# The seam ahead of attention reordered, and both groups of scores side by side in five passes

## The chip, the cores and the metric

The kernel runs on one core of a Trainium2 chip. The metric is the device time of one execution in microseconds (us), the median of three runs. A core has these engines: PE (matrix products and transposes), ACT (ScalarE), DVE (VectorE), POOL (GpSimd) and SP (SyncE, which here issues transfers). PEld is PE's loading of weights. PE writes its results into PSUM, eight banks of 128 x 512 fp32; ACT and DVE read them there.

## The reference

It is a two-layer decoder trunk on 512 positions of width 1024 in fp32. The layer ahead is a short gated convolution with a SwiGLU feed-forward block. Then one shared pair of keys and values is projected, and the second layer is attention over a sliding window of 128 positions with sinks, followed by another SwiGLU block. Only the parts around the change:

```python
kv = rmsnorm(h, kv_norm) @ w_kv                    # 4 key heads and 4 value heads of 64
k_sh, v_sh = jnp.split(kv, 2, axis=-1)
k_sh = partial_rotary(k_sh, cos, sin)
q = partial_rotary(rmsnorm(h, b_pre_norm[j]) @ b_w_q[j], cos, sin)      # 16 heads of 64
scores = einsum('bnqhgd,bnkhd->bnhgqk', qb, kk) / sqrt(64)              # window of 128
scores = where(valid, scores, -1e30)
probs = softmax(concatenate([scores, sink]))[..., :-1]
attn = einsum('bnhgqk,bnkhd->bnqhgd', probs, vv) @ b_w_o[j]
h = h + rmsnorm(attn, b_post_norm[j])
ff = swiglu(rmsnorm(h, ffn_pre_norm[l]), ffn_w_gate_up[l], ffn_w_down[l])
h = h + rmsnorm(ff, ffn_post_norm[l])
```

## The kernel before

**Products.** Every fp32 operand is split into a high and a low part, and every product is made as three (`mm3`, L191 to L194: low with high, high with high, high with low). So a step of the contraction is a group of three matmuls. The sequence is worked on in four tiles of 128 positions (t = 0 to 3), and in two halves of 256 columns (hf) where the positions lie along the free axis. The model's width is eight chunks of 128 (f or k = 0 to 7).

**Order.** In the stages around the change all engines run exactly the order in which the code is written (`tc.manual_schedule`). Waits between engines are added by the framework from what each instruction reads and writes. Buffers of PSUM come from three pools: `ps_mm` (four banks, handed round in turn), `ps_sc` (two) and `ps_pt` (two).

**The seam.** `close` (L869) makes the down projection that ends the first feed-forward block (`ffn(0)`). While the last half of the last tile is worked on (`pmix`, four k, twelve matmuls), it does two of the four k, then the transposes of the first two tiles, then the other two k. The residual update `res` follows each tile: `res.norm(t)` (L326) makes the normalised rows `xn` on ACT; `res.turn(b, ts)` (L328) transposes on PE the chunks b and b+4 of the tiles ts into one bank (`xt`, L337), a bank for each b of 0 to 3 and each half hf; `res.split(n, f, hf)` (L340) makes the high part on ACT (`xhi`, L350) and the low part on DVE (`xlo`, L351) from that bank, for the keys and values (n = 0) and, with another gain, for the queries (n = 1). For f < 4 and n = 0 both lie in a tile named `xhl`. Chunks f and f+4 therefore are read from the same bank, `banks[f % 4, hf]`.

`last_tile` (L909) orders ACT and DVE around the last tile's update; its list `pieces` says which splits (n, f) of the first half stand at which of five places in it. The fourth place is ahead of `res.norm(3)`, the fifth behind it. Then PE projects keys (`pk`) and values (`pv`) over k = 0 to 7 for the first half, and turns the second half's tiles (2, 3) behind k=6 and k=7; those transposes go into the banks from which the first half's splits read.

**Attention.** It runs in ten passes i = 0 to 9, each through the steps of the string `ORDER`, software-pipelined: S0 and S1 are the two groups of scores of pass i (`scores(half)`, two tiles of positions each), each twelve matmuls on half of the array's rows (`psc`, L1306), M their maxima, E exponents, N normalising; T, P, L turn the probabilities of the pass before (`pt`, L1363) and split them, W weighs the values (`po`), O is the output; Q projects the queries two passes ahead (`pq`), R- rotates them (L1244 to L1248), H- splits them into `rhl` (L1253 on ACT, L1254 on POOL); K and k rotate and split the second pair of key heads (`rhi`, `rlo`; only in passes 2 and 3); Z and z multiply with the output weights (`pe`). A step name with a minus belongs to the instance started a pass earlier. Pass i starts with S0; in the profile these starts are at 548.58, 556.35, 568.60, 580.59, 592.58, 604.58, 622.01 and 634.00 for i = 0 to 7.

Of the kernel before, what the change touches and what calls it, by code (L numbers as in the profile page):

```python
# [44 lines left out]

EARLY_IN, REST_IN = 2, 0
ORDER = (
    "R- S0 T0 T1 O- Q0 M0 Q1 Z0 P0 P1 S1 T2 T3 L0 Q2 L1 G K M1 E00 E01 H- k g0 Q3 P2 P3 E10 E11 Z1 z0 W0 L2 L3 A A A N0 W1 W2 N1 W3 g1 z1"
)
STEP = {  # L50
    "S": "scores", "M": "maxima", "E": "exponents", "N": "normalise", "T": "turn", "P": "high",
    "L": "low", "W": "weigh", "O": "out", "Q": "project", "R": "rotate", "H": "split",
# [21 lines left out]
def yoco_kernel(  # L74
# [32 lines left out]
    ps_mm = ctx.enter_context(tc.tile_pool(name="ps_mm", bufs=4, space=PSUM))  # L107
# [448 lines left out]
    for l in range(2):  # L556
# [3 lines left out]
        for rd, (f0, f1) in enumerate(ROUNDS[:-1]):  # L560
            k = slice(f0 // 2, f1 // 2)
# [304 lines left out]
        if square:  # L866
            res.square(t)

    def close(ws, x, k0, res, ahead, then=None, each=2):  # L869


        n = len(x) - k0

        def part(ps, t, half, ks):
            unit(ps, t, ws[len(ws) // 2 * half :], x, ks, n, k0)

        begun = [bank("pmix", ps_mm) for _ in range(2)]
        for half in range(2):
            part(begun[half], 0, half, range(n - 1))
            for _ in range(each if half == 0 or each > 1 else 0):  # L880
                ahead.one()
        for t in range(NB):
            for half in range(2):
                if t == 0:
                    ps = begun[half]
                    part(ps, t, half, range(n - 1, n))
                else:
                    ps = bank("pmix", ps_mm)
                    if (t, half) == (NB - 1, 1):
                        part(ps, t, half, range(2))  # L890
                        for b in range(4):
                            res.turn(b, (0, 1))
                        part(ps, t, half, range(2, n))
                        for f in range(4):
                            res.split(0, f, 0)
                        res.square_mix(t, 0)
                        res.square(NB - 2)
                        res.scale(t, 0)
                    else:
                        part(ps, t, half, range(n))  # L900
                res.take(t, half, ps)
                if (t, half) != (NB - 1, 0):
                    res.square_mix(t, half)
            if t < NB - 1:
                tile_done(res, t, square=t < NB - 2)
            if t == 0 and then:
                then()
# [56 lines left out]
    def ffn(l, before, ahead, gain, gpres, following):  # L964
# [220 lines left out]
        if gpres:  # L1185
            ahead = Ahead(following)
            with tc.manual_schedule(engines=ALL):
                close(ws, acts[-1], 0, res, ahead)
            return res, ahead
        with tc.manual_schedule(engines=ALL):  # L1190
            for t in range(NB):
# [88 lines left out]
    class Heads:  # L1280
# [11 lines left out]
        def scores(self, half):  # L1292
            khi, klo = ks[self.t // 4]
            qhi, qlo = qs[self.t].hi, qs[self.t].lo
            self.pss[half] = pss = [bank("psc", ps_sc) for _ in range(2)]
            for i, cc in self.spans(half):
                n = 2 * half + i
                q = slice(n * P, (n + 1) * P)

                kk = slice(max(n - 1, 0) * P, max(n + 1, 2) * P)  # L1300
                cc = slice(i * 256, (i + 1) * 256)
                rows = [slice(e * HD, (e + 1) * HD) for e in range(2)]

                for i, (x, y) in enumerate(((qhi, klo), (qhi, khi), (qlo, khi))):
                    for e, r in enumerate(rows):
                        nc.tensor.matmul(pss[e][:, cc], x[r, q], y[r, kk], start=i == 0,  # L1306
                                         stop=i == 2)
# [118 lines left out]
    at = []  # L1426

    with tc.manual_schedule(engines=ALL):
        last_tile(res, [[(0, 4)], [(0, 5)], [], [(0, 6), (0, 7), (1, 0), (1, 1)],
                        [(1, f) for f in (4, 5, 2, 3, 6, 7)]])  # L1430
        for hf in range(2):
            c = slice(hf * 256, (hf + 1) * 256)
            for k in range(KT):
                kk = slice(k * P, (k + 1) * P)
                for ps, (whi, wlo) in zip(pk, wk):
                    mm3(ps[:, c], whi[:, kk], wlo[:, kk], xkv[k][0][:, c], xkv[k][1][:, c],
                        k == 0, k == KT - 1)
                values(2 * hf, k)
                values(2 * hf + 1, k)
                if hf == 0 and k >= 6:  # L1440
                    for b in (2 * k - 12, 2 * k - 11):
                        res.turn(b, (2, 3))
                        res.split(0, b, 1)
            if hf == 0:
                for f in range(4, KT):
                    res.split(0, f, 1)
            if hf == 0:
                ahead.one()
                for f in range(KT):
                    res.split(1, f, 1)  # L1450
                ahead.one()
                qs[0].w, qs[1].w = ahead.ready[4:]


        vt = [halves("vt", F32R) for _ in range(NB)]
        for pair in vt:
            for v in pair:
                nc.gpsimd.memset(v.bitcast(F32), 0.0)

        last_p = [slot("lp", F32R) for i in range(2)]  # L1460
        for p in last_p:
            nc.gpsimd.memset(p.bitcast(F32), 0.0)
        for part in range(4):
            qs[0].project(part)
        ks = [rope_split(rope(pk[0], nc.vector), nc.vector)]
        qs[LEAD].weights()
        nc.scalar.activation(warm, ones[:, 0:1], AF.Exp)
        for part in range(4):
            qs[1].project(part)
        qs[0].rotate(nc.vector)  # L1470
        qs[0].split(nc.vector)
        dst = [[v.rearrange("p (h d) -> p h d", d=2 * HD)[:, :, :HD] for v in pair]
               for pair in vt]
        src = [p.rearrange("p (h d) -> p h d", d=HD) for p in pv]
        for j in range(NB):
            nc.scalar.activation(dst[j][0], src[j], AF.Copy)
        for j in range(NB):
            nc.vector.tensor_tensor(out=dst[j][1], in0=src[j], in1=dst[j][0].bitcast(F32),
                                    op=ALU.subtract)

    with tc.manual_schedule(engines=ALL):
        sum_on("a0")
        for i in range(KT + 2):
            if i == KT:
                res = Update(mix_o, B_ATT, [G_FPRE[1]])
                res.leaves = True
                ahead = Ahead(first_weights(1))
            if i == KT + 1:
                res.load()
            for c in ORDER.split():  # L1490
                if c == "A":
                    if i == KT:
                        ahead.one()
                    continue
                if c == "K":
                    if i == 2:
                        rot_k = rope(pk[1], nc.gpsimd)
                    continue
                if c == "k":
                    if i == 3:  # L1500
                        ks.append(rope_split(rot_k, nc.gpsimd))
                    continue
                late = c.endswith("-")
                op, n = c[0], [int(d) for d in c[1:].rstrip("-")]
                t = i - late
                if op == "g":

                    u = 2 * (t - EARLY - 1) + n[0]
                    if u in (-2, -1, 2, 3):
                        j = u + 2 if u < 0 else u  # L1510
                        early_w.append(split_weights(w_o[j // 2, j % 2], slots=j >= EARLY_IN))
                    continue
                if op in "SMENTPLWO":
                    t -= op in "TPLWO"
                    of = hp
                elif op in "QRH":
                    t += LEAD
                    of = qs
                elif op == "G":
                    t += LEAD + 1  # L1520
                    of = qs
                    if KT <= t < KT + 4:
                        j = t - KT
                        rest_w.append(split_weights(w_o[j // 2, 2 + j % 2], slots=j >= REST_IN))
                else:
                    t = 2 * (t - EARLY - 1) + n.pop(0)
                    of = early
                if 0 <= t < len(of) and not (op in "RH" and t < LEAD - 1):
                    getattr(of[t], STEP[op])(*n)
                if op in "RH" and i <= KT:  # L1530
                    issue(len(issues) // 2 if op == "R" else len(issues))
            if i <= KT:
                sum_on(f"a{i + 1}")
# [97 lines left out]
```

## Time and profile before

| what | value |
|---|---|
| median of three runs | 1020.13 us (1019.88 to 1020.14) |
| the profiled execution's own time | 1020.08 us |
| its span | 1018.3 us, 16274 instructions |
| granted clock of PE | 0.999 of full speed |
| busy: PE, PEld | 1009.6 us (99%), 892.7 us (88%) |
| busy: DVE, ACT, POOL | 867.5 us (85%), 581.2 us (57%), 194.6 us (19%) |
| the seam | 508 to 526 us of the span |
| attention, passes 0 to 7 | 548.6 to 644 us |

A row of the timeline gives start, duration, engine, line, operation, what it writes and reads, shapes, how many neighbours are folded into it, and in square brackets how long the engine was idle before it and what ended that. Ends of matmuls are modelled and overlap, so the distance from one start to the next is the price of a matmul. Rows of the view by windows give, for each stretch, its length and each engine's busy time. Reading ACT's or DVE's idle time needs care: PE has hardly any, and idle time of the others costs nothing unless PE waits for them.

### The profile page before, as it was taken

The numbers are of one execution on the slowest core, as the hardware profiler recorded it, in microseconds if no ns is written. First come the engines' busy times: TensorE is split into PE (matmuls) and PEld (weight loads), VectorE is DVE, ScalarE is ACT, GpSimd is POOL, SyncE is SP. The second block draws the span as 40 slices with busy tenths as digits, with TensorE's granted clock in tenths as the row PEclk, the third lists the DMA queues.
The fourth block names the chain that finished last, engine by engine and source line by source line (L and its number), as shares of the span: only waits on it lengthen the run. The fifth ranks groups of instructions, "written<-read, shape, count | busy, mean of one in ns | idle before, by whom it ended". The sixth has DMA issues, their size and how long they took to land.

```text
span 1018.3 us, 16274 instructions
## 1 busy us (share of the span) xinstructions
PE 1009.6 (99%) x6008; PEld 892.7 (88%) x6008; DVE 867.5 (85%) x1480; ACT 581.2 (57%) x1035; POOL 194.6 (19%) x259
## 2 busy tenths in 40 slices
PE   9999999999999999999999999999999999999997
PEld 8888888999889898998898888889998998989986
DVE  5766767899789999998869998778997899999896
ACT  6322444875655555566566776677666564645641
POOL 0443033102101011000122653221111010110001
PEclk9999999999999999999999999999999999999999
DMA  9997789549979699779504889976899576979742
GB/s 355 288 269 220 183 257 344 158 166 279 343 239 297 216 298 334 234 219 324 183 2 141 205 243 273 246 278 151 270 291 330 169 245 233 284 273 273 245 164 83
DMA packets 66575, 244.50 MB, mean 240 GB/s; under 512 B 7872, under 2 KB 8384, under 8 KB 54720
## 3 DMA queue, kind: packets, MB, share of 16 engines
q1 hardware_dynamic: 51328, 145.98, 38.8%
q0 software_dynamic: 14592, 96.48, 37.5%
q8 instruction: 47, 0.77, 0.3%
q10 hardware_dynamic: 576, 1.02, 0.3%
q14 instruction: 32, 0.26, 0.1%
HBM read 237.15 MB, written 102.76 MB: 334 GB/s over the span
## 4 chain that ended last, share of the span: by engine, by line
PE 93%; DVE 3%; ACT 2%; issue 1%; DMA 0%; POOL 0%; DVEq 0%; SPq 0%; ACTq 0%
PE gx L1055 14%; PE gx L1058 7%; PE pcub L194 4%; PE pcub L192 4%; PE pcub L193 4%; PE gz L194 4%; PE gz L193 4%; PE gz L192 4%; PE px L192 3%; PE px L193 3%; PE px L194 3%; PE pmix L193 2%; PE pmix L192 2%; PE pmix L194 2%; PE gy L194 2%; PE gy L193 2%
## 5 line engine op out<-in xcount | busy, mean ns | idle before, releaser
L478 DVE TENSOR_TENSOR wlo<-raw,whi 128x1024 fp32r<-128x1024 f32 x225 | 274.6, 1225 | 53.1 <-ACT whi L477 53.0
L477 ACT ACTIVATE whi<-raw 128x1024 fp32r<-128x1024 f32 x225 | 233.6, 1050 | 102.3 <-DVE raw L465 28.7
L1055 PE MATMUL gx<-xt,whi 128*128 128x512 f32 x480 | 120.4, 393 | 0.0
L1055 PEld LDWEIGHTS gx<-xt,whi 128*128 128x128 f32 x480 | 86.3, 189 | 15.5
L546 POOL DMA_DIRECT2D hsum<-in_w_gb_dram x96 | 62.8, 735 | 151.0 <-ACT whi L477 90.2
L546 POOL DMA_DIRECT2D hsum<-hsum x32 | 25.2, 789 | 294.3 <-ACT whi L477 219.3
L1017 DVE TENSOR_TENSOR st<-gx,st 128x256 f32<-128x256 f32 x200 | 77.9, 419 | 2.6 <-ACT st L1033 0.5
L1033 ACT ACTIVATE st<-gx 128x256 f32<-128x256 f32 x120 | 43.2, 380 | 62.6 <-PE gx L1058 58.9
L1058 PEld LDWEIGHTS gx<-xt,wlo 128*128 128x128 f32 x480 | 65.5, 190 | 4.7
L1058 PE MATMUL gx<-xt,wlo 128*128 128x256 f32 x480 | 66.9, 282 | 0.0
L1069 ACT ACTIVATE gr<-gr 128x1024 f32<-128x1024 f32 x20 | 21.3, 1063 | 50.1 <-DVE gr L1017 50.1
L192 PE MATMUL px<-wlo,ahi 128*128 128x512 f32 x120 | 46.8, 390 | 0.1
L194 PE MATMUL px<-whi,alo 128*128 128x512 f32 x120 | 46.7, 389 | 0.0
L193 PE MATMUL px<-whi,ahi 128*128 128x512 f32 x120 | 46.7, 389 | 0.0
L194 PE MATMUL gz<-xhi,wlo 128*128 128x256 f32 x160 | 45.5, 284 | 0.0
L193 PE MATMUL gz<-xt,whi 128*128 128x256 f32 x160 | 45.3, 283 | 0.0
L192 PE MATMUL gz<-xt,whi 128*128 128x256 f32 x160 | 45.3, 283 | 0.0
L193 PE MATMUL gy<-xhi,whi 128*128 128x256 f32 x160 | 45.3, 283 | 0.0
L192 PE MATMUL gy<-xlo,whi 128*128 128x256 f32 x160 | 45.3, 283 | 0.0
L194 PE MATMUL gy<-xhi,wlo 128*128 128x256 f32 x160 | 45.3, 283 | 0.0
L192 PE MATMUL gz<-xlo,whi 128*128 128x256 f32 x160 | 45.3, 283 | 0.0
L194 PE MATMUL gz<-xt,wlo 128*128 128x256 f32 x160 | 45.3, 283 | 0.0
(298 smaller groups left out, 2991.7 us busy)
## 6 DMA issues: line engine op xcount, KB each, us to landing
hsum<-in_w_gb_dram POOLq DMA_DIRECT2D x96, 512.0 KB, 7.9
raw<-hsum SPq DMA_DIRECT2D x88, 512.0 KB, 8.1
raw<-in_w_gb_dram SPq DMA_DIRECT2D x60, 512.0 KB, 7.1
hsum<-in_w_dn_dram POOLq DMA_DIRECT2D x36, 512.0 KB, 8.4
raw<-in_w_dn_dram SPq DMA_DIRECT2D x32, 512.0 KB, 6.3
hsum<-hsum POOLq DMA_DIRECT2D x28, 512.0 KB, 5.6
raw<-in_w_in_dram SPq DMA_DIRECT2D x21, 512.0 KB, 7.8
hsum<-in_w_dn_dram POOLq DMA_DIRECT2D x12, 768.0 KB, 13.1
```

The costliest lines, as they stand in the source:

```text
L192: nc.tensor.matmul(out, whi, xlo, start=start, stop=False, **kw)
L193: nc.tensor.matmul(out, whi, xhi, start=False, stop=False, **kw)
L194: nc.tensor.matmul(out, wlo, xhi, start=False, stop=stop, **kw)
L477: self.begun = nc.scalar.activation(hi[:, :n], raw, AF.Copy)
L478: nc.vector.tensor_tensor(out=lo[:, :n], in0=raw, in1=hi[:, :n].bitcast(F32), op=ALU.subtract)
L546: nc.gpsimd.dma_start(dst, src, max_dma_last_dim=4 * 4 * S, **kw))
L1017: nc.vector.tensor_tensor(out=out, in0=a, in1=b, op=ALU.add)
L1033: nc.scalar.activation(ste, a, AF.Copy)
L1055: nc.tensor.matmul(banks[c][e], whi[:, kk], factors[p][k][2], start=opened and k == 0, stop=False, **kw)
L1058: nc.tensor.matmul(banks[c][e][:, :256], wlo[:, kk], factors[p][k][0], start=False, stop=k == 3 and p == 4, **kw)
L1069: nc.scalar.activation(kept[2], kept[2], AF.Silu)
```

## The change

It has four parts. In attention, S1 stands right behind S0 in the passes of `NEXT`, and its two banks then come from `ps_mm`; and step k stands ahead of H-, which only pass 3 notices. In the seam, three of the last four k (instead of two) stand ahead of the first transposes, and the splits and the second half's transposes have another order.

```diff
 ORDER = (
-    "R- S0 T0 T1 O- Q0 M0 Q1 Z0 P0 P1 S1 T2 T3 L0 Q2 L1 G K M1 E00 E01 H- k g0 Q3 P2 P3 E10 E11 Z1 z0 W0 ..."
+    "R- S0 T0 T1 O- Q0 M0 Q1 Z0 P0 P1 S1 T2 T3 L0 Q2 L1 G K M1 E00 E01 k H- g0 Q3 P2 P3 E10 E11 Z1 z0 W0 ..."
 )
+NEXT = (0, 3, 4, 6, 7)
...
-    def close(ws, x, k0, res, ahead, then=None, each=2):
+    def close(ws, x, k0, res, ahead, then=None, each=2, lead=2):
...
-                        part(ps, t, half, range(2))
+                        part(ps, t, half, range(lead))
                         for b in range(4):
                             res.turn(b, (0, 1))
-                        part(ps, t, half, range(2, n))
+                        part(ps, t, half, range(lead, n))
...
-                close(ws, acts[-1], 0, res, ahead)
+                close(ws, acts[-1], 0, res, ahead, lead=3)
...
-            self.pss[half] = pss = [bank("psc", ps_sc) for _ in range(2)]
+            pool = ps_mm if half and self.t in NEXT else ps_sc
+            self.pss[half] = pss = [bank("psc", pool) for _ in range(2)]
...
-        last_tile(res, [[(0, 4)], [(0, 5)], [], [(0, 6), (0, 7), (1, 0), (1, 1)],
-                        [(1, f) for f in (4, 5, 2, 3, 6, 7)]])
+        last_tile(res, [[(0, 4)], [(0, 5)], [], [(0, 6), (0, 7), (1, 0), (1, 4)],
+                        [(1, f) for f in (1, 5, 2, 6, 3, 7)]])
...
                 if hf == 0 and k >= 6:
-                    for b in (2 * k - 12, 2 * k - 11):
+                    for b in ((0,), (1, 2, 3))[k - 6]:
                         res.turn(b, (2, 3))
                         res.split(0, b, 1)
...
-            for c in ORDER.split():
+            order = ORDER
+            if i in NEXT:
+                order = order.replace("S1 ", "").replace("S0 ", "S0 S1 ")
+            for c in order.split():
```

What stands in a row on ACT around `res.norm(3)` in the seam, before: the `xn` row is that norm, the rows are the splits (1,0), (1,1), then (1,4), (1,5), (1,2), (1,3), (1,6), (1,7); the name behind the arrow with `xt` is the bank's content, and the bracket says where the program makes ACT wait.

```order
L350 ACTIVATE xhi_5249<-xt_5168,gt 128x256
L350 ACTIVATE xhi_5253<-xt_5173,gt 128x256 [waits DVE_49]
L326 ACTIVATE xn_5257<-h_5000,ur_4990 128x1024 [waits Pool_49]
L350 ACTIVATE xhi_5259<-xt_5168,gt 128x256 [waits DVE_49]
L350 ACTIVATE xhi_5263<-xt_5173,gt 128x256 [waits DVE_49]
L350 ACTIVATE xhi_5267<-xt_5178,gt 128x256
L350 ACTIVATE xhi_5271<-xt_5183,gt 128x256
L350 ACTIVATE xhi_5275<-xt_5178,gt 128x256 [waits DVE_49]
L350 ACTIVATE xhi_5279<-xt_5183,gt 128x256 [waits DVE_49]
```

The same place now:

```order
L351 ACTIVATE xhi_5249<-xt_5171,gt 128x256
L351 ACTIVATE xhi_5253<-xt_5171,gt 128x256 [waits DVE_49]
L327 ACTIVATE xn_5257<-h_5000,ur_4990 128x1024 [waits Pool_49]
L351 ACTIVATE xhi_5259<-xt_5176,gt 128x256
L351 ACTIVATE xhi_5263<-xt_5176,gt 128x256 [waits DVE_49]
L351 ACTIVATE xhi_5267<-xt_5181,gt 128x256
L351 ACTIVATE xhi_5271<-xt_5181,gt 128x256 [waits DVE_49]
L351 ACTIVATE xhi_5275<-xt_5186,gt 128x256
L351 ACTIVATE xhi_5279<-xt_5186,gt 128x256 [waits DVE_49]
```

Each bank now is read twice in succession, the `xn` row stands behind the first second reader, and the second reader of each bank carries the wait for DVE; before, the second readers stood two places or more behind the first.

On PE in pass 3, the way into S1 before: a group of `pq` products (Q1), then the first scores of S1.

```order
L193 MATMUL pq_6146<-xhi_5271,whi_6021 128x512
L194 MATMUL pq_6146<-xhi_5271,wlo_6022 128x512
L1306 MATMUL psc_6168<-rlo_5583,rhl_6046 128x256
L1306 MATMUL psc_6169<-rlo_5583,rhl_6046 128x256
L1306 MATMUL psc_6168<-rhi_5582,rhl_6046 128x256
```

The same scores now, behind the last two of S0 (`psc_6115` and `psc_6116` are S0's banks, `psc_6129` and `psc_6130` S1's):

```order
L1308 MATMUL psc_6115<-rhi_5582,rhl_6046 128x256
L1308 MATMUL psc_6116<-rhi_5582,rhl_6046 128x256
L1308 MATMUL psc_6129<-rlo_5583,rhl_6046 128x256
L1308 MATMUL psc_6130<-rlo_5583,rhl_6046 128x256
L1308 MATMUL psc_6129<-rhi_5582,rhl_6046 128x256
L1308 MATMUL psc_6130<-rhi_5582,rhl_6046 128x256
```

S1's twelve rows have moved ahead of the transposes T0 and T1 and of the projections Q0 and Q1; nothing else on PE in this pass changes its place.

On POOL in pass 3, the split of the next queries (`rhl`), two weight transfers (`hsum`) and the split of the second key pair (`rlo`), before:

```order
L1248 TENSOR_TENSOR ra_6110<-ra_6110,sh_6108 128x512
L546 DMA hsum_179<-hsum_178 64x2048
L1254 TENSOR_TENSOR rhl_6221<-ra_6110,rhl_6221 128x512
L546 DMA hsum_182<-in_w_gb_dram 64x2048
L546 DMA hsum_183<-in_w_gb_dram 64x2048
L1254 TENSOR_TENSOR rlo_6227<-ra_6027,rhi_6226 128x512
L1247 TENSOR_TENSOR sh_6287<-sh_6287,stab_5217 128x512
```

and now:

```order
L1249 TENSOR_TENSOR ra_6110<-ra_6110,sh_6108 128x512
L547 DMA hsum_179<-hsum_178 64x2048
L1255 TENSOR_TENSOR rlo_6222<-ra_6027,rhi_6221 128x512
L1255 TENSOR_TENSOR rhl_6225<-ra_6110,rhl_6225 128x512
L547 DMA hsum_182<-in_w_gb_dram 64x2048
L547 DMA hsum_183<-in_w_gb_dram 64x2048
L1248 TENSOR_TENSOR sh_6287<-sh_6287,stab_5217 128x512
```

The `rlo` row has moved ahead of `rhl` and of both transfers; on ACT the matching two rows, `rhl` and `rhi`, are swapped. The orders of DVE and SP are unchanged but for the banks' names.

More of the change, by code (lines that the diff above doesn't have):

```diff
@@ L47 @@
 ORDER = (
-    "R- S0 T0 T1 O- Q0 M0 Q1 Z0 P0 P1 S1 T2 T3 L0 Q2 L1 G K M1 E00 E01 H- k g0 Q3 P2 P3 E10 E11 Z1 z0 W0 L2 L3 A A A N0 W1 W2 N1 W3 g1 z1"
+    "R- S0 T0 T1 O- Q0 M0 Q1 Z0 P0 P1 S1 T2 T3 L0 Q2 L1 G K M1 E00 E01 k H- g0 Q3 P2 P3 E10 E11 Z1 z0 W0 L2 L3 A A A N0 W1 W2 N1 W3 g1 z1"
 )
+NEXT = (0, 3, 4, 6, 7)
 STEP = {
```

## The prediction

> **What bounds the kernel now.** I read the page first, then the waits of TensorE (PE), then the timeline of the two places that the change touches. The page says whose time it is:
>
> ```profile
> PE 1009.6 (99%) x6008; PEld 892.7 (88%) x6008; DVE 867.5 (85%) x1480; ACT 581.2 (57%) x1035; POOL 194.6 (19%) x259
> ```
>
> PE works almost without a gap, so the time is PE's own work plus its few waits. Beside one at the start, the view of waits lists two, both on the transposes (`xt`, L337) of the seam:
>
> ```profile
> PE xt L337 <- DVE xlo L351: 0.2, 1, 0.2
> PE xt L337 <- ACT xn L326: 0.2, 1, 0.2
> ```
>
> No wait of PE stands in the feed-forward block behind attention, so I carry what PE gains or loses in seam and attention through to the end unchanged. What a wait costs is read from starts in the timeline, since ends of matmuls are modelled.
>
> ```profile
> 508.83 0.27 PE L337 MATMUL xt<-ident,xn 128*128 128x128 f32 x1
> 509.32 1.86 PE L337 MATMUL xt<-ident,xn 128*128 128x128 f32 x15 [0.21 <-ACT xn L326]
> ...
> 522.34 0.28 PE L194 MATMUL pv<-whi,xlo 128*128 128x256 f32 x1
> 522.86 1.07 PE L337 MATMUL xt<-ident,xn 128*128 128x128 f32 x8 [0.24 <-DVE xlo L351]
> ...
> 525.20 1.04 PE L337 MATMUL xt<-ident,xn 128*128 128x128 f32 x8
> 525.99 0.36 PE L192 MATMUL pk<-xhl,whi 128*128 128x256 f32 x1
> ```
>
> One transpose takes about 0.11 (15 in 1.86, the last's tail included). The first wait costs 0.49 − 0.11 = 0.38, the second 0.52 − 0.12 = 0.40, 0.12 being the pitch of the 256-column products. In the seam ACT makes `xhi` from a bank of transposes and DVE then makes `xlo` from the same bank and that `xhi`:
>
> ```profile
> 519.73 1.66 DVE L351 SCALAR_TENSOR_TENSOR xlo<-xt,gt,xhi 128x256 fp32r<-128x256 f32 x4 [0.21 <-ACT xhi L350]
> 519.25 1.55 ACT L350 ACTIVATE xhi<-xt,gt 128x256 fp32r<-128x256 f32 x4
> 520.67 1.16 ACT L326 ACTIVATE xn<-h,ur 128x1024 f32<-128x1024 f32 x1
> 521.71 1.58 ACT L350 ACTIVATE xhi<-xt,gt 128x256 fp32r<-128x256 f32 x4
> 522.23 1.66 DVE L351 SCALAR_TENSOR_TENSOR xlo<-xt,gt,xhi 128x256 fp32r<-128x256 f32 x4 [0.84 <-ACT xhi L350]
> 523.53 0.87 ACT L350 ACTIVATE xhi<-xt,gt 128x256 fp32r<-128x256 f32 x2 [0.24 <-DVE xlo L351]
> 524.04 0.88 DVE L351 SCALAR_TENSOR_TENSOR xlo<-xt,gt,xhi 128x256 fp32r<-128x256 f32 x2 [0.15 <-ACT xhi L350]
> L351 DVE SCALAR_TENSOR_TENSOR xlo<-xt,gt,xhi x16: 474/478/487, 516.4 to 528.4; 128x256 fp32r<-128x256 f32 x16
> L350 ACT ACTIVATE xhi<-xt,gt x16: 453/476/512, 515.9 to 527.7; 128x256 fp32r<-128x256 f32 x16
> ```
>
> The sixth row is the one that matters: ACT's split of (1,6) waits 0.24 for DVE's split of (1,2). It needs no result of it; the two read one bank. So the program lets ACT and DVE read a bank only in turn. Different banks run in parallel: four in 1.55 on ACT, a pitch of 0.36, and four in 1.66 on DVE, a pitch of 0.39.
>
> **The change, part by part.**
>
> *Pieces and turns in the seam.* Splits f and f+4 share a bank. Before, they stand apart; now (1,0) (1,4), (1,1) (1,5), (1,2) (1,6), (1,3) (1,7) follow each other, and each pair is a ping-pong: ACT 0.48, DVE 0.48, ACT of the partner. With 0.03 a hand-off (DVE's row of 519.73 begins its first split 0.48 behind ACT's of 519.25), ACT's partner starts 1.02 behind the first, and the next pair's first 0.36 behind that; in the chain below DVE is in the way once for another 0.04: 1.42 per pair, where DVE alone needs 2 × 0.39 = 0.79. From the rows: DVE's (1,0) is the third of the four from 519.73 and runs 520.52 to 521.00; nothing ahead of it is changed on ACT or DVE. ACT's (1,4) starts at 521.03; it stood fourth in the row of 519.25, at 520.31. Behind it `xn` of the last tile moves from 520.67 to 521.39 and ends at 522.55 (duration 1.16). ACT's (1,1) starts at 522.43 (1.04 after `xn`, as before), (1,5) at 523.45, (1,2) at 523.80, (1,6) at 524.86, (1,3) at 525.22, (1,7) at 526.28; DVE ends (1,5) at 524.43, (1,6) at 525.85, (1,7) at 526.28 + 0.48 + 0.03 + 0.48 = 527.27. Before, the last ended at 524.92 (524.04 + 0.88).
>
> Who waits for it is PE: the transposes of the second half overwrite these banks, one b after the other. Turn b=0 now waits for `xn` until 522.6; four transposes and the products of k=7 follow and take 1.9 (before, eight transposes and these products took 2.34, 522.86 to 525.20; four transposes are 0.44), until 524.5, just as DVE leaves bank 1. Turn b=2 then waits for 525.85 and b=3 for 527.27. With 0.06 to 0.15 of start (the transposes of 522.86 started 0.15 behind the DVE split that they waited for, the first of the four of 522.23) and 0.40 for four transposes, the next `pk` starts at 527.73 to 527.82 instead of 525.99. **Term: +1.75**, with bounds 1.5 (all six splits that are left at the shortest of the L350 and L351 rows, no hand-off) and 2.1 (all at the longest, 0.06 a hand-off).
>
> *lead=3* puts three more products of 512 columns, some 0.68, ahead of the first transposes, which covers the 0.38. But turn b=0 waits for ACT and then b=3 for DVE, whose times hang on the chain above, and this does not start earlier: PE arrives early and waits longer. The 0.38 and the 0.40 are inside the +1.75. Worth 0 here; without the ping-pong the two waits gone would be −0.78.
>
> *Scores side by side.* The second group, S1, runs in another tiling of the array (64\*128 in the rows) than its neighbours (128\*128):
>
> ```profile
> 584.73 0.39 PE L193 MATMUL pq<-xhi,whi 128*128 128x512 f32 x1
> 584.95 0.39 PE L194 MATMUL pq<-xhi,wlo 128*128 128x512 f32 x1
> 585.27 0.38 PE L1306 MATMUL psc<-rlo,rhl 64*128 64x256 f32 x2
> 585.50 0.40 PE L1306 MATMUL psc<-rhi,rhl 64*128 64x256 f32 x4
> ...
> 585.85 0.40 PE L1306 MATMUL psc<-rhi,rhl 64*128 64x256 f32 x4
> 586.17 0.87 PE L1363 MATMUL pt<-ident,s 128*128 128x128 f32 x6
> 586.80 0.48 PE L192 MATMUL pq<-xlo,whi 128*128 128x512 f32 x1
> ...
> 649.79 0.39 PE L194 MATMUL pe<-whi,ohl 128*128 128x512 f32 x1
> 650.03 0.81 PE L1363 MATMUL pt<-ident,s 128*128 128x128 f32 x6
> 650.60 0.48 PE L192 MATMUL pe<-wlo,ohl 128*128 128x512 f32 x1
> ```
>
> Going in, 0.32 lie between 584.95 and 585.27 where a product takes 0.22, and 0.23 between the first two pairs where a pair takes 0.117 (three pairs from 585.50 to 585.85). Coming out, the last pair (585.97) to 586.17 is 0.20, and six transposes take 0.63 against 0.57 at 650.03 without a switch. From the last product to the second transpose that is 1.385 now; without the switches it is 0.24 + 0.11 + 6 × 0.115 = 1.04. **Saved: 0.35 in each of passes 3, 4, 6 and 7, 1.4 together.** In pass 0 S1 stands between two projections:
>
> ```profile
> 552.15 0.39 PE L194 MATMUL pq<-xhi,wlo 128*128 128x512 f32 x1
> 552.47 0.39 PE L1306 MATMUL psc<-rlo,rhl 64*128 64x256 f32 x2
> 553.37 0.51 PE L192 MATMUL pq<-xlo,whi 128*128 128x512 f32 x1
> 553.71 0.40 PE L193 MATMUL pq<-xhi,whi 128*128 128x512 f32 x1
> ```
>
> 552.15 to 553.71 is 1.56; without switches 0.23 + 0.69 + 0.23 = 1.15, so 0.41. Whether PE can use them depends on DVE:
>
> ```profile
> 548.60:556.40 7.80, 7.80 (x51) 5.91 (x50) 7.73 (x28) 4.67 (x19) 5.90 (x7) 1.00 0.16 60
> 580.60:592.60 12.00, 12.00 (x89) 10.35 (x88) 11.82 (x39) 8.88 (x28) 7.16 (x8) 1.00 0.96 200
> 592.60:604.60 12.00, 12.00 (x89) 10.34 (x88) 11.86 (x39) 10.27 (x29) 7.47 (x9) 1.00 0.67 166
> 622.00:634.00 12.00, 12.00 (x87) 10.34 (x86) 10.49 (x35) 10.99 (x34) 3.96 (x5) 1.00 0.95 230
> ...
> 582.34 0.48 PE L192 MATMUL pq<-xlo,whi 128*128 128x512 f32 x1
> 582.36 0.68 DVE L1246 TENSOR_TENSOR ra<-pq,ctab 128x512 f32<-128x512 f32 x1
> 580.26 0.15 DVE L1346 TENSOR_TENSOR se<-se,rs 128x4 f32<-128x4 f32 x1
> 589.78 1.05 DVE L1346 TENSOR_TENSOR se<-se,rs 128x4 f32<-128x4 f32 x1
> ```
>
> The columns behind the length are PE, PEld, DVE, ACT and POOL busy. In pass 0 DVE has 0.07 to spare, and pass 1 follows at once; I count 0.03 of the 0.41 (bounds 0 and 0.41). In passes 3 and 4 DVE is busy for 11.82 and 11.86 of 12.00, more than the 11.65 that PE will need. I still count them whole, since 0.9 of pass 3's DVE time is one short operation (589.78: 1.05, elsewhere 0.15) held while POOL works on `rlo`, which the next part moves, and pass 6 leaves 1.5; the low bound is 0.18 + 0.14 for these two.
>
> *Banks.* S1 takes two of the four buffers of the pool that holds the projections. In pass 3 the projection Q0, which starts at 582.34, comes six pairs of scores later, at 583.03, and gets the bank that DVE's rope (582.36 + 0.68) reads until 583.04: some 0.07 of wait, bounds 0 and 0.35. *k ahead of H-* (pass 3 only): POOL makes `rlo` ahead of `rhl` and two weight transfers (1.31 later), ACT swaps `rhi` and `rhl`. PE needs neither before the next pass, where S0 starts at 592.6; DVE may gain 0.9. Worth 0 on PE, and 0 to −0.1 at the bounds.
>
> The sum: +1.75 − 1.41 − 0.03 + 0.07 = **+0.38**. The profiled execution took 1020.08, so 1020.46; against the median of 1020.13 it is 1020.5.
>
> **A rule weighed.** The row that decides the seam is ACT's 0.24 behind DVE at 523.53. The Trainium skill, "PSUM — Partial Sum Buffer", section "PSUM bank collisions raise a hardware error", says that two engines must not access one bank in the same partitions at once, two reads included, and that software has to keep them apart. By that rule the pairs must alternate, the trace agrees with its one 0.24, and the sum is +0.38; were the wait only an accident of this one place, the sum would be case A.
>
> **The rivals.** 0.2% is 2.04, about what a measurement of this kernel can tell from no change.
>
> *A, faster, 0.15:* the partner's wait does not reach PE, so that both waits of the seam vanish: −0.78 − 1.41 + 0.04 = −2.15 (0.04: banks less pass 0), with pass 0's whole 0.41 −2.5: 1017.6 to 1018.0. For it: only one such wait is in the trace, of 0.24. Against: it is served in the order of the program, and now four pairs in a row have it.
>
> *B, slower, 0.17:* DVE becomes the second bound in attention. Its place is Q0 of pass 3: PE arrives 0.35 earlier than before, DVE does not, and the rope that frees the bank ends 0.35 later relative to PE; the same holds for whatever reads DVE's results in passes 4, 6 and 7. All of 1.41 comes back as waits, and Q0 adds 0.35: +1.75 + 0.35 = +2.1, with the upper bounds +2.6: 1022.2 to 1022.7. It decides from the point at which DVE, busy for 98% in passes 3 and 4, falls behind by more than the 0.9 that POOL gives back. Against it: pass 6 has room.
>
> *C, 0.06:* ping-pong and removed waits cancel in the seam, the rest gives −1.37: 1018.8, within the 0.2%.
>
> **How the numbers follow.** The forecast has 0.62, with a range of its own of 1019.7 (1.5 − 1.41 − 0.41 − 0.1) to 1021.5 (2.1, less 0.18 + 0.14 + 0.71 of scores, plus 0.35 of banks). It and C lie within 0.2%: 0.68. A gives faster 0.15, B slower 0.17. The range reaches down to C and up to the middle of B, 1018.6 to 1022.4, and leaves out A and the end of B.
>
> **What would show it.** In the new trace: the first `pk` of the second half some 1.75 later than the first transposes' time predicts, PE's waits for `xlo` at b=2 and b=3 of about 1.0 each, ACT's waits for `xlo` in every pair; no wait at the first transposes; 24 scores in a row with one way in and one way out, and passes 3, 4, 6, 7 of 11.65. Wrong would be: PE's waits in the seam under 0.5 together (A), or new waits of PE for DVE in attention of over 1 together (B).

## The result, and the profile after

The changed kernel takes 1021.7 us (median of 22 runs, 1020.97 to 1022.84) against 1020.13 us for the kernel before (22 runs, 1019.78 to 1022.34): a ratio of 1.0014 with an interval of 1.0008 to 1.0019. It is a little slower, by 0.8 to 1.9 us, which is less than the 0.2% that the prediction takes for no change, and the time lies within the stated range. The waits of PE in the changed kernel:

```profile
PE xt L338 <- DVE xlo L352: 1.6, 2, 0.8
PE idle L676 <- DVE ones L142: 1.1, 1, 1.1
PE pt L1365 <- DVE s L1353: 0.3, 1, 0.3
```

The second row stands at the start of the program, far from the change. The wait of the first transposes for ACT's `xn` is gone, the one for DVE's `xlo` has become two of 0.8, and one is new, of the probabilities' transposes (`pt`) for DVE's normalising (`s`). The seam in the timeline of the changed kernel, ACT first, then DVE, then PE:

```profile
521.53 0.47 ACT L351 ACTIVATE xhi<-xt,gt 128x256 fp32r<-128x256 f32 x1 [0.60 <-DVE xlo L352]
521.90 1.14 ACT L327 ACTIVATE xn<-h,ur 128x1024 f32<-128x1024 f32 x1
...
523.96 0.84 ACT L351 ACTIVATE xhi<-xt,gt 128x256 fp32r<-128x256 f32 x2 [0.55 <-DVE xlo L352]
525.38 0.84 ACT L351 ACTIVATE xhi<-xt,gt 128x256 fp32r<-128x256 f32 x2 [0.58 <-DVE xlo L352]
526.80 0.47 ACT L351 ACTIVATE xhi<-xt,gt 128x256 fp32r<-128x256 f32 x1 [0.58 <-DVE xlo L352]
...
525.89 0.88 DVE L352 SCALAR_TENSOR_TENSOR xlo<-xt,gt,xhi 128x256 fp32r<-128x256 f32 x2 [0.54 <-ACT xhi L351]
527.30 0.48 DVE L352 SCALAR_TENSOR_TENSOR xlo<-xt,gt,xhi 128x256 fp32r<-128x256 f32 x1 [0.54 <-ACT xhi L351]
...
522.67 0.97 PE L338 MATMUL xt<-ident,xn 128*128 128x128 f32 x4
...
525.10 0.63 PE L338 MATMUL xt<-ident,xn 128*128 128x128 f32 x4
526.52 0.63 PE L338 MATMUL xt<-ident,xn 128*128 128x128 f32 x4 [0.79 <-DVE xlo L352]
527.93 0.63 PE L338 MATMUL xt<-ident,xn 128*128 128x128 f32 x4 [0.79 <-DVE xlo L352]
528.32 0.36 PE L193 MATMUL pk<-xhl,whi 128*128 128x256 f32 x1
```

Every second reader of a bank waits 0.55 to 0.60 on ACT for DVE, and DVE waits 0.54 for ACT in turn. A pair takes 1.42 (523.96, 525.38, 526.80), and PE's turns b=1, 2 and 3 follow each other at the same 1.42 (525.10, 526.52, 527.93). Four transposes alone take 0.44, so by the starts each of the two waits costs 0.98. This execution was 0.48 later than the one of before ahead of the seam, where the two kernels are alike, so `pk` stands at 527.84 on the clock of before, where it was 525.99: **+1.85**.

Per stretch, worked out from starts of PE in the timelines: the seam from one product of the first feed-forward block (at 446.11 in before) to the first scores of pass 0, then each pass from S0 to S0, and from S0 of pass 7 to a product 2000 matmuls ahead of the end. The kernels of the experiments are explained below.

| kernel | to S0 of pass 0 | pass 0 | 1 | 2 | 3 | 4 | 5 | 6 | 7 and on |
|---|---|---|---|---|---|---|---|---|---|
| before | 102.46 | 7.77 | 12.24 | 11.99 | 11.99 | 11.99 | 17.43 | 11.99 | 52.35 |
| changed | 104.32 | 7.28 | 12.74 | 11.99 | 11.70 | 11.78 | 17.43 | 11.89 | 52.21 |
| e1 seam only | 104.33 | 7.77 | 12.23 | 11.99 | 11.99 | 11.99 | 17.43 | 11.99 | 52.35 |
| e2 attention only | 102.46 | 7.28 | 12.72 | 11.99 | 11.71 | 11.77 | 17.43 | 11.89 | 52.20 |
| e3 old pieces | 102.46 | 7.28 | 12.73 | 11.99 | 11.70 | 11.79 | 17.43 | 11.89 | 52.20 |
| e4 spread pieces | 101.82 | 7.77 | 12.24 | 11.99 | 11.70 | 11.79 | 17.43 | 11.89 | 52.19 |
| e5 no swap | 102.47 | 7.28 | 12.72 | 11.99 | 11.69 | 12.33 | 17.43 | 11.87 | 52.20 |
| e6 lead only | 102.48 | 7.77 | 12.24 | 11.99 | 11.99 | 11.99 | 17.43 | 11.99 | 52.35 |
| e7 pass 0 only | 102.49 | 7.28 | 12.72 | 11.99 | 11.99 | 11.99 | 17.43 | 11.99 | 52.35 |
| e8 pass 5 as well | 101.81 | 7.77 | 12.27 | 11.99 | 11.70 | 11.79 | 18.52 | 11.89 | 52.20 |
| e9 weights later | 101.79 | 7.77 | 12.22 | 11.99 | 11.70 | 11.70 | 18.74 | 11.70 | 54.34 |
| e10 swap only | 102.44 | 7.78 | 12.23 | 11.99 | 11.99 | 11.99 | 17.43 | 11.99 | 52.32 |

The changed kernel loses 1.86 in the seam. Pass 0 gains 0.49 and pass 1 loses 0.50. Passes 3, 4, 6 and 7 gain 0.29, 0.21, 0.10 and 0.14, together 0.74. The balance is +1.13. The stretch ahead of the seam differs from execution to execution (that product starts between 445.67 and 446.60 in all but e10, where it is 447.85), which is why the table is read rather than the spans.

### The profile page after: what moved, and what is told of

Same layout as the page of the kernel before. It is cut to its first block, busy times and chain, and to the rows that moved or that the text cites. A ratio compares the mean times of both kernels' runs of the same rounds, so it can differ in the third digit from the quotient of the medians.

```text
span 1020.0 us, 16262 instructions
## 1 busy us (share of the span) xinstructions
PE 1009.8 (99%) x6008; PEld 893.4 (88%) x6008; DVE 868.4 (85%) x1480; ACT 582.1 (57%) x1035; POOL 194.1 (19%) x259
## 4 chain that ended last, share of the span: by engine, by line
PE 91%; DVE 5%; ACT 2%; issue 1%; POOL 0%; DVEq 0%; ACTq 0%
PE gx L1056 14%; PE gx L1059 7%; PE pcub L194 4%; PE pcub L195 4%; PE pcub L193 4%; PE gz L195 4%; PE gz L194 4%; PE gz L193 4%; PE px L193 3%; PE px L195 3%; PE px L194 3%; PE pmix L194 2%; PE pmix L193 2%; PE pmix L195 2%; PE gy L194 2%; PE gy L193 2%
```

## The experiments

Of each kernel the time is the median of 11 runs, the ratio is to the kernel before with its interval. Line numbers are those of the changed kernel.

**e1, the seam alone.**

```diff
-NEXT = (0, 3, 4, 6, 7)
+NEXT = ()
-    "... E01 k H- g0 ..."
+    "... E01 H- k g0 ..."
```

> The seam as changed (three k ahead of the first transposes, the pairs (1,f) (1,f+4) next to each other, turn b=0 behind k=6 and b=1 to 3 behind k=7), attention as before. Theory (the ping-pong of ACT and DVE on one bank costs 1.86 in the seam, attention gave back 0.73): the first scores come 1.8 to 1.9 later against the start of the seam, and the time is 1020.1 + 1.85 = 1022.0. Rival (the seam's loss is made up again ahead of attention): first scores unchanged, 1020.1 to 1020.5.

1022.1 us, ratio 1.0018 (1.0009 to 1.0026). The first scores are 1.87 later, every pass is that of before, and nothing is made up.

**e2, attention alone.** The pieces, the turns and `lead` are those of before.

> Attention as changed (both groups of scores side by side in passes 0, 3, 4, 6, 7; k ahead of H-), the seam as before. Theory: passes 3, 4, 6 and 7 are 0.3, 0.2, 0.1 and 0.1 shorter, what pass 0 gains is a wait in pass 1; 1020.1 - 0.7 = 1019.4. Rival (DVE is the bound in attention and the shorter passes of the changed kernel came only from the later seam): 1019.9 to 1020.2.

1019.3 us, ratio 0.9994 (0.9985 to 1.0003): the interval takes in no change, so the reading rests on the passes. They are those of the changed kernel within 0.02: the gain of 0.75 in passes 3, 4, 6 and 7 does not need the later seam, and the loss of e1 and this gain add up to the whole change.

**e3, the old pieces in the changed kernel.**

```diff
-        last_tile(res, [[(0, 4)], [(0, 5)], [], [(0, 6), (0, 7), (1, 0), (1, 4)],
-                        [(1, f) for f in (1, 5, 2, 6, 3, 7)]])
+        last_tile(res, [[(0, 4)], [(0, 5)], [], [(0, 6), (0, 7), (1, 0), (1, 1)],
+                        [(1, f) for f in (4, 5, 2, 3, 6, 7)]])
```

> The changed kernel with the splits in the order of before, so that the banks alternate; lead=3 and the new order of the turns stay. Theory (the order of the pieces is the whole loss): turn b=0 waits for DVE's (1,4) until 522.9 as before, b=1 and b=2 do not wait, b=3 by about 0.3; the seam comes out 0.35 earlier than before, and with 0.7 of attention the time is 1019.1. Rival (three turns in a row behind k=7 are the loss): about 1.0 to 1.3 of wait stays and the time is 1020.5 to 1021.0.

1019.58 us, ratio 0.9993 (0.9985 to 1.0002). The seam is 102.46, exactly that of before: the whole loss is the order of the pieces, and with the old pieces the new order of the turns costs nothing. The 0.35 expected as a gain did not come. Two waits of PE in e3, and rows of its seam:

```profile
PE xt L338 <- DVE xlo L352: 0.7, 1, 0.7
PE pt L1365 <- DVE s L1353: 0.3, 1, 0.3
...
524.16 0.88 DVE L352 SCALAR_TENSOR_TENSOR xlo<-xt,gt,xhi 128x256 fp32r<-128x256 f32 x2 [0.15 <-ACT xhi L351]
...
522.04 0.28 PE L195 MATMUL pv<-whi,xlo 128*128 128x256 f32 x1
522.98 0.63 PE L338 MATMUL xt<-ident,xn 128*128 128x128 f32 x4 [0.66 <-DVE xlo L352]
...
526.11 0.36 PE L193 MATMUL pk<-xhl,whi 128*128 128x256 f32 x1
```

Turn b=0 waits for DVE's (1,4) as before, and from there to `pk` PE has the same work in either order without another wait (3.13 in e3, 522.98 to 526.11, and 3.13 before, 522.86 to 525.99); there was nothing left to gain.

**e4, pieces far apart and all turns behind k=7.** Pass 0 is left as it was.

```diff
-NEXT = (0, 3, 4, 6, 7)
+NEXT = (3, 4, 6, 7)
-        last_tile(res, [[(0, 4)], [(0, 5)], [], [(0, 6), (0, 7), (1, 0), (1, 4)],
-                        [(1, f) for f in (1, 5, 2, 6, 3, 7)]])
+        last_tile(res, [[(0, 4)], [(0, 5)], [],
+                        [(0, 6), (0, 7), (1, 0), (1, 1), (1, 2), (1, 3)],
+                        [(1, f) for f in (4, 5, 6, 7)]])
-                    for b in ((0,), (1, 2, 3))[k - 6]:
+                    for b in ((), (0, 1, 2, 3))[k - 6]:
```

> The changed kernel with the splits of the queries in the order (1,0) (1,1) (1,2) (1,3), then xn of the last tile, then (1,4) to (1,7), with all four turns behind k=7, and with passes 3, 4, 6 and 7 only. Theory: every bank's second reader comes four places behind the first, each turn finds its bank free, PE does not wait in the seam at all; the seam is 0.7 shorter than before, attention 0.7, so 1018.7. Rival (DVE's split of the second half then comes too late for the first pk, or PE waits for xn): seam gain under 0.3, 1019.1 or more.

1018.75 us, ratio 0.9986 (0.9977 to 0.9995): faster than both kernels. Its seam in the timeline:

```profile
519.14 2.29 ACT L351 ACTIVATE xhi<-xt,gt 128x256 fp32r<-128x256 f32 x6
521.28 1.18 ACT L327 ACTIVATE xn<-h,ur 128x1024 f32<-128x1024 f32 x1
522.32 1.60 ACT L351 ACTIVATE xhi<-xt,gt 128x256 fp32r<-128x256 f32 x4
...
519.63 2.44 DVE L352 SCALAR_TENSOR_TENSOR xlo<-xt,gt,xhi 128x256 fp32r<-128x256 f32 x6 [0.21 <-ACT xhi L351]
522.86 1.66 DVE L352 SCALAR_TENSOR_TENSOR xlo<-xt,gt,xhi 128x256 fp32r<-128x256 f32 x4 [0.79 <-ACT xhi L351]
...
523.49 1.94 PE L338 MATMUL xt<-ident,xn 128*128 128x128 f32 x16
525.20 0.38 PE L193 MATMUL pk<-xhl,whi 128*128 128x256 f32 x1
```

With four splits between the two readers of a bank no second reader waits on ACT, and all sixteen transposes run in one row without a wait. The seam is 0.64 shorter than before (101.82). The run changes two things at once, the pieces and the place of the turns, and does not part them. An estimate from the rows of e3: with the old pieces and all four turns behind k=7, PE would come to the turns near 523.7 (twelve products of 0.12 behind 522.04), wait some 0.1 for DVE's (1,6) and start `pk` near 525.6 instead of 526.11. About 0.5 of the 0.64 would then be the place of the turns, and only the rest the spread. This was not tried.

**e5, without the swap of k and H-.** As e2, with

```diff
-    "... E01 k H- g0 ..."
+    "... E01 H- k g0 ..."
```

> Attention as changed in the five passes, but k behind H- as before; the seam as before. Theory (the swap only shortens a hold of DVE by POOL in pass 3 and PE does not feel it): the times of e2 within 0.1, pass 3 11.70 long, DVE's short L1348 operation behind lp in pass 3 takes about 1 again. Rival (the 0.9 of DVE was what let PE use the shorter pass 3): pass 3 or 4 is 0.2 to 0.3 longer than in e2 (11.70 and 11.78).

1020.3 us, ratio 1.0003 (0.9994 to 1.0012). The theory was wrong and the rival right, by more than it asked: pass 4 is 12.33 instead of 11.77. The execution of e5 is 0.22 later than that of e2 at the start of pass 3. DVE and POOL at the end of pass 3, and PE in pass 4, in e5:

```profile
589.57 1.62 DVE L1348 TENSOR_TENSOR se<-se,rs 128x4 f32<-128x4 f32 x1
...
589.86 1.30 POOL L1255 TENSOR_TENSOR rlo<-ra,rhi 128x512 fp32r<-128x512 f32 x1
...
594.47 0.67 DVE L1247 TENSOR_TENSOR ra<-pq,ctab 128x512 f32<-128x512 f32 x1
...
595.20 0.50 PE L193 MATMUL pq<-xlo,whi 128*128 128x512 f32 x1 [0.36 <-DVE ra L1247]
```

and the same places in e2:

```profile
589.35 0.54 DVE L1348 TENSOR_TENSOR se<-se,rs 128x4 f32<-128x4 f32 x1
...
588.59 1.28 POOL L1255 TENSOR_TENSOR rhl<-ra,rhl 128x512 fp32r<-128x512 f32 x1
...
593.16 0.69 DVE L1247 TENSOR_TENSOR ra<-pq,ctab 128x512 f32<-128x512 f32 x1
...
594.39 0.48 PE L193 MATMUL pq<-xlo,whi 128*128 128x512 f32 x1
```

Without the swap the short operation on DVE (`se`) lasts until POOL's `rlo` ends (1.62); with it, until POOL's `rhl` ends (0.54). DVE's rope of pass 4 (`ra`) ends at 595.14 instead of 593.85, later by the 0.22 of the execution and by the 1.08 that `se` is longer, and the projection Q0, whose bank that rope reads, waits for it.

**e6, lead=3 alone.**

> Only lead=3; all the rest as before. Theory (the 0.38 is swallowed by the wait of turn b=0 for DVE's (1,4), which hangs on ACT and DVE alone): the first transposes start without a wait, those behind k=6 wait 0.6 instead of 0.24 by the view of waits, the first pk of the second half keeps its place, and the time is that of before: 1020.0. Rival (PE's gain goes through): 0.38 less, 1019.6.

1020.33 us, ratio 1.0002 (0.9994 to 1.0011), seam 102.48. The only wait of the seam in e6:

```profile
PE xt L338 <- DVE xlo L352: 0.7, 1, 0.7
```

The wait of the transposes for `xn` is gone, and the other grew from 0.2 to 0.7: the gain is swallowed, as the theory has it.

**e7, pass 0 alone.** `NEXT = (0,)`, all the rest as before.

> Only pass 0 has both groups side by side; all the rest as before. Theory (DVE sets the end of pass 0 and 1): pass 0 is 0.49 shorter, pass 1 0.48 longer by a wait of PE for DVE's normalising, the time is that of before: 1020.0. Rival (the wait of pass 1 has its cause in the later passes or the seam): 0.4 less.

1020.15 us, ratio 1.0001 (0.9992 to 1.0011). Pass 0 gains 0.49, pass 1 loses 0.48. PE's new wait, in e7 as in the changed kernel:

```profile
PE pt L1365 <- DVE s L1353: 0.3, 1, 0.3
```

**e8, pass 5 as well.** As e4, with `NEXT = (3, 4, 5, 6, 7)`.

> As e4, with pass 5 side by side as well. Theory (each pass gives 0.3, less what DVE is late; pass 5 is 17.4 long with 14.2 of DVE): pass 5 is 0.25 to 0.3 shorter and the whole 0.2 to 0.3 faster than e4. Rival (S1's banks from the projections' pool make PE wait in pass 5, which has no query projection but the output's products): pass 5 as before or longer, no gain over e4.

1019.77 us, ratio 0.9998 (0.9990 to 1.0007). Pass 5 becomes 1.09 longer; the rival was right, though its remark that pass 5 has no query projection was not. DVE and PE in pass 5 of e8:

```profile
604.35 1.22 DVE L189 TENSOR_TENSOR wlo<-raw,whi 128x1024 fp32r<-128x1024 f32 x1
605.49 0.72 DVE L1245 STREAM_SHUFFLE sh<-pq 128x512 f32<-128x512 f32 x1
606.11 0.67 DVE L1247 TENSOR_TENSOR ra<-pq,ctab 128x512 f32<-128x512 f32 x1
...
606.83 0.50 PE L193 MATMUL pq<-xlo,whi 128*128 128x512 f32 x1 [1.12 <-DVE ra L1247]
```

Q0 again waits for the rope that reads its bank, 1.12 here, since the rope stands behind a weight split. Time on the average (14.2 of 17.4 for DVE) said nothing of this place.

**e9, the weights' split behind L3.** As e4, with

```diff
-    "... H- g0 Q3 P2 P3 E10 E11 Z1 z0 W0 L2 L3 A A A ..."
+    "... H- Q3 P2 P3 E10 E11 Z1 z0 W0 L2 L3 g0 A A A ..."
```

> As e4, with step g0 (the split of a piece of the output weights, wlo on DVE) behind L3 instead of ahead of Q3; this moves wlo behind plo and lp on DVE in passes 4 and 6. Theory (the 0.1 and 0.2 that W waits in passes 4 and 6 are for plo, which stands behind wlo in DVE's queue): pass 4 becomes 11.70 and pass 6 11.70 long, W's waits go, the whole is 0.2 to 0.3 faster than e4. Rival (the weights are then late for the output's products, or DVE only shifts the wait to the next pass's T1 or Q0): no gain, or a new wait of PE on wlo.

1021.95 us, ratio 1.0018 (1.0009 to 1.0027). Passes 4 and 6 become 11.70, as the theory has it, so the 0.1 and 0.2 that they lacked were W's wait for `plo` behind `wlo` on DVE. But pass 5 grows by 1.31 and the last stretch by 2.15, through waits of the transposes for DVE in e9:

```profile
PE pt L1365 <- DVE plo L1382: 1.2, 1, 1.2
...
PE pt L1365 <- DVE s L1353: 0.9, 3, 0.4
```

Pushed behind `plo`, the weights' split stands ahead of the normalising, and PE waits for that. By the starts of PE against e4, pass 5 loses 1.3 at the transposes that wait for the normalised `s`; the last stretch loses some 0.7 in the same way and 1.4 at the one that waits for `plo`. Moving the split in one pass alone was not tried.

**e10, the swap alone.**

> Only k ahead of H-, all the rest as before. Theory (with pass 3 at its old length the rope of pass 4 is early enough with either order): passes as before, 11.99 each, time as before. Rival (the hold of DVE by POOL costs PE something in the kernel before as well): pass 4 shorter than 11.99.

1020.07 us, ratio 1.0004 (0.9995 to 1.0013). All passes are those of before within 0.03: the swap is worth nothing while pass 3 has its old length, and 0.56 in pass 4 once pass 3 is shorter (e2 against e5).

## Why the prediction was right or wrong, point by point

- **The seam, +1.75: right.** It measured +1.86. The mechanism is shown by the changed kernel against e3, which differ in the order of the splits alone: next to each other the seam is 104.32 and ACT's waits are 0.55 to 0.60, two apart it is 102.46 with one wait of 0.24. Four apart (e4) ACT has no such wait; its seam of 101.82 is also due to the turns' place. The waits of PE at b=2 and b=3, expected at about 1.0 each, cost 0.98 each by the starts. The period of 1.42 per pair was met. The rule of the Trainium skill, "PSUM — Partial Sum Buffer", section "PSUM bank collisions raise a hardware error" (readers of one bank on two engines have to be kept apart), stands behind these rows: no two such reads of one bank overlap in the rows shown.
- **lead=3 swallowed: right** (e6), and the second wait of the seam too; 0.64 of their 0.78 come back in e4, where PE comes to the turns only when the banks are free.
- **Pass 0 lost: right** (e7). Pass 0 itself gives 0.49, and pass 1 takes 0.48 back through DVE's normalising.
- **The scores, −1.41: mis-sized, −0.74 measured.** The cost of the way in and out is nearly as worked out: in pass 3, where nothing else waits, PE gains 0.33 from S0 to the first product behind the second transposes (6.21 before, 580.59 to 586.80, and 5.88 now, 582.93 to 588.81), and the whole pass is 0.29 shorter, instead of 0.35. The step that failed is "I still count them whole" for passes 4, 6 and 7, which gave 0.21, 0.10 and 0.14. There PE reaches W (passes 4 and 6) or the second transposes (pass 7) before DVE is done with `plo`. In pass 6 of the changed kernel:

```profile
631.47 1.98 DVE L183 TENSOR_TENSOR wlo<-raw,whi 128x512 fp32r<-128x512 f32 x2 [0.58 <-ACT whi L182]
633.37 0.68 DVE L1382 TENSOR_TENSOR plo<-pt,phi 128x512 fp32r<-128x512 f32 x1
...
633.89 0.28 PE L195 MATMUL po<-phi,vt 128*128 128x256 f32 x1
634.11 0.39 PE L193 MATMUL po<-plo,vt 128*128 128x256 f32 x1
634.33 0.28 PE L194 MATMUL po<-phi,vt 128*128 128x256 f32 x1
```

  Two pitches of 0.22 instead of 0.12 cost 0.2, right behind the end of `plo` at 634.05. Pass 6 was taken as safe because DVE is idle for 1.5 of it; that idle time lies elsewhere, 0.58 of it ahead of `wlo`, for ACT. That these waits hang on `plo` behind `wlo` is shown by e9: with `wlo` behind `plo` both passes are 11.70. This is the mild form of rival B. Too small for the view of waits, it shows only in the starts.
- **The banks, +0.07 in pass 3: the mechanism right, place and size not.** Pass 3 shows no such wait. The place where Q0 and the rope meet is pass 4 without the swap (e5, 0.36 by the row) and pass 5 (e8, 1.12).
- **The swap "worth 0 on PE": wrong.** The 0.9 of DVE in pass 3 was named as the reason to count the scores whole, and then the edit that frees it was costed at nothing. Alone it is nothing (e10), but with the shorter pass 3 it carries 0.56. The Trainium skill, "SBUF — State Buffer", section "Who interferes with whom", says that a DVE instruction with two SBUF inputs contends with a GpSimd instruction that reads SBUF, and that the order of issue decides which of the two is held. The trace fits in that `se` ends with POOL's `rlo` in e5 (589.57 + 1.62 and 589.86 + 1.30, some 0.03 apart) and with `rhl` in e2 (589.35 + 0.54 and 588.59 + 1.28, some 0.02 apart). In e2 `rhl` starts ahead of `se`, but in e5 `se` is listed as starting ahead of `rlo`, so who issued first cannot be read from it.
- **The sum.** −1.41 instead of −0.74 is 0.67 of the 0.75 between the forecast of +0.38 and the balance of +1.13; the seam adds 0.11, pass 0 some 0.04, and the 0.07 of the banks did not come. That the medians differ by 1.6 instead of 1.1 stays open; their interval (0.8 to 1.9) takes in both, and the fastest runs of the two kernels differ by 1.19. The measured 1021.7 lies just above the forecast's own range, which ends at 1021.5; it is inside the stated range because that reaches into rival B. Two sums of the prediction are slightly off: four times 0.35 is 1.40, and B's bounds add up to 2.1 + 0.35 = 2.45, not 2.6.

## What to carry to other kernels

When two engines read results from one bank in turn, put the other banks' readers between them. Next to each other, a pair cost 1.42 here: ACT's two splits (0.84), DVE's one between them (0.48) and two hand-offs of some 0.05. Apart, it costs only the slower engine's two pitches of 0.39. Time won by a bound engine is kept only as far as the next place at which another engine's result is needed, so look for the row that ends last at that place, not at the other engine's idle time over the pass. An edit that frees an engine that nobody waits for is worth nothing alone and can be what lets another edit pay: try such edits together and apart.

## What the runs showed of the hardware that was not expected

A 128x4 operation on DVE, 0.15 long by itself, took up to 1.62 while POOL worked on a 128x512 one (e5). The switch of PE between scores on 64 rows and products on 128 costs about 0.2 on the way in and 0.15 on the way out, by the prediction's rows of pass 3 (in: 0.32 for 0.22 and 0.23 for 0.117; out: 0.20 for 0.117 and 0.63 for 0.57); with one way in and one way out less, those rows of pass 3 are 0.33 shorter. The 24 scores in a row kept their pitch: from S0's start to the next transposes pass 3 now has 1.62, where S0 alone has 0.91 in pass 2, which is as it was (570.93 to 571.84), so S1 adds 0.71, six pairs of 0.118. The rows of the changed kernel, pass 2 first:

```profile
570.93 0.39 PE L1308 MATMUL psc<-rlo,rhl 64*128 64x256 f32 x2
...
571.84 0.33 PE L1365 MATMUL pt<-ident,s 128*128 128x128 f32 x1
...
582.93 0.39 PE L1308 MATMUL psc<-rlo,rhl 64*128 64x256 f32 x2
...
584.55 0.33 PE L1365 MATMUL pt<-ident,s 128*128 128x128 f32 x1
```
